# The last stage of a hybrid decoder step: accumulators, order of the second half, and how the final norm and its stores are placed

## The chip, the cores and the metric

The kernel runs on one core of one Trainium2 chip. Its engines are TensorE (PE in the profile, its weight loads PEld), VectorE (DVE), ScalarE (ACT), GpSimd (POOL) and SyncE (SP), which here only issues DMAs. The metric is the time of one execution on the device in microseconds; lower is better. Three runs of the kernel before gave 1003.35, 1006.09 and 1006.34 us, a median of 1006.09.

## The reference, cut to what matters

One step of a decoder layer over 512 prompt tokens and 8 sample tokens, 520 in all, with 1024 features: a SwiGLU feed-forward, a mixer (pooling and a state space model), a second SwiGLU feed-forward, and a last RMS norm. The change lies in the end of the second feed-forward and in the norm:

```python
h = h + 0.5 * _swiglu(_rms_norm(h, ffn2_norm), ffn2_w_gate, ffn2_w_up, ffn2_w_down)
...
return _rms_norm(h, final_norm), ...

def _rms_norm(x, g):
    y = x * rsqrt(mean(x * x, axis=-1) + EPS)
    return y * g
```

The mean runs over the 1024 features of a token, so no token of the output is known before all its features are.

## The kernel before, in words

Features lie on the 128 partitions, in 8 tiles `d` = 0 to 7 of 128 features each (`KD`); tokens lie along a row, in two halves `b` of 260 tokens (`HB`). Products are made to nearly fp32 precision by splitting both operands into a high and a low part and taking three matmuls (`mm3`, lines 116 to 119).

The feed-forward's 2816 inner features are 22 tiles, taken in chunks of 8, 8 and 6. For each chunk `rest` (lines 318 to 338) makes the gated products `g` and then multiplies them with the down-projection. For the last chunk this is `down_by_half` (lines 392 to 432): it loads and splits the weights of all eight output tiles (lines 395 to 406), and then goes through the tokens' first half and after it the second half. For each half and each output tile `part(d, b, ks)` does 6 x 3 matmuls into an accumulator `dh` in PSUM (line 417), and `done(d, b)` takes it out on DVE: line 422 scales it into `th` and line 424 adds it to `h`. Three tiles of the first half are begun without the last of the six inner tiles, while that one is still being made (lines 427 and 428).

PSUM has eight banks here: tag `ps` with two banks, tag `A` with two, and tag `BE` with two tiles of two banks. In `part` the output tiles 0 and 1, and 4 and 5, share one `BE` tile; tiles 2, 3, 6 and 7 have an `A` bank each. A buffer is given to its next user when the reads of all that was in it are done.

After each output tile `after2(d, b, hs)` (lines 526 to 538) prepares the norm. ACT squares the new `h` (`sumsq`, lines 141 to 148), DVE adds the square to `acc_last`, and ACT writes `hg`, which is `h` times the norm's gain (line 536). For the very last tile the square `sq_last` isn't added on DVE but given to TensorE, and DVE makes `hg` (lines 529 to 533). When the eighth tile of a half is through, `finish(b)` (lines 540 to 554) sums `acc_last` over the partitions with a matmul by a matrix of ones into `psl`, ACT takes the square root (line 546), and then, for each quarter of 130 tokens, DVE takes the reciprocal (line 550) and multiplies four tiles at a time (line 552), and SP stores each product (line 554): four stores of 260 KB a half, in runs of 130 floats.

The order of instructions on each engine isn't the program's. A scheduler works it out ahead of time from its own estimates of durations: what it takes to be ready first goes first, and program order decides between what is ready. `tc.keep_in_program_order(x)` sets one bound for it: `x` is issued behind the instruction that the program has just ahead of it on the same engine. On the chip each engine then works through its list in order.

Of the kernel before, what the change touches and what calls it, by code (L numbers as in the profile page):

```python
# [9 lines left out]
F32 = mybir.dt.float32  # L10
F32R = mybir.dt.float32r
AF = mybir.ActivationFunctionType
ALU = mybir.AluOpType
# [3 lines left out]
P = 128  # L17
D = 1024
# [3 lines left out]
HB = NT // 2  # L22
HALVES = (slice(0, HB), slice(HB, NT))
KD = D // P
# [38 lines left out]
def tile_trunk_step(ctx: ExitStack, tc: tile.TileContext, ins: dict, outs: dict):  # L63
    nc = tc.nc
# [7 lines left out]
    tmp = ctx.enter_context(tc.tile_pool(name="tmp", bufs=3, side="right"))  # L72
    dr = ctx.enter_context(tc.tile_pool(name="dr", bufs=1, space=DRAM))
    ps = [None]

    def bank(name):
        return ps[0].tile([P, 512], F32, tag="ps", name=name)
# [3 lines left out]
    h = vx[:, NVEC:].rearrange("p (d t) -> p d t", d=KD)  # L81

    def v(name, i, n=P):
        return vec[:n, VEC[name] + i : VEC[name] + i + 1]

    ones = cst.tile([P, P], F32, tag="ones", name="ones")
    nc.vector.memset(ones, 1.0)
    eps = cst.tile([P, 1], F32, tag="eps", name="eps")
# [7 lines left out]
    def raw_tile(name):  # L96
        if not half:
            t = raw_pair(name)
            half.extend([t[:, 1], t[:, 0]])
        return half.pop()  # L100

    def split(src, n, name, hp, nb, tags):
        hi, lo = (hp.tile([P, 1024], F32R, tag=t, bufs=nb, name=f"{t}_{name}")[:, :n] for t in tags)
        h, l = hi, lo
        if len(src.shape) == 3:
            h, l = (t.rearrange("p (j c) -> p j c", j=src.shape[1]) for t in (hi, lo))
        nc.scalar.copy(h, src)  # L107
        nc.vector.tensor_tensor(out=l, in0=src, in1=h.bitcast(F32), op=ALU.subtract)
        return hi, lo
# [3 lines left out]
        nc.sync.dma_start(out=raw, in_=src)  # L113
        return split(raw, n, name, wp, 3, ("whi", "wlo"))

    def mm3(ps, whi, wlo, xhi, xlo, start, stop, **kw):
        nc.tensor.matmul(ps, whi, xhi, start=start, stop=False, **kw)  # L117
        nc.tensor.matmul(ps, whi, xlo, start=False, stop=False, **kw)  # L118
        nc.tensor.matmul(ps, wlo, xhi, start=False, stop=stop, **kw)  # L119

    def ws(w, k, m=P):
        return w[:, k * m : (k + 1) * m]
# [18 lines left out]
    def sumsq(acc, d, hs, name):  # L141
        n = hs.stop - hs.start
        if d == 0:
            nc.scalar.activation(out=acc[:, hs], in_=h[:, d, hs], func=AF.Square)
        else:
            sq = tmp.tile([P, HB], F32, tag="ta", name=f"sq_{name}_{d}")
            nc.scalar.activation(out=sq[:, :n], in_=h[:, d, hs], func=AF.Square)
            nc.vector.tensor_tensor(out=acc[:, hs], in0=acc[:, hs], in1=sq[:, :n], op=ALU.add)
# [47 lines left out]
    class Ffn:  # L196
# [153 lines left out]
        def down(self, c, lo, hi, after):  # L350
# [3 lines left out]
            def part(d, ks):  # L354
                if d not in units:
                    units[d] = load_unit(ins[f"w{self.i}d"][d, :, lo * P : hi * P], n * P, f"{self.i}d{d}_{c}")
                    banks[d] = ps[0].tile([P, 2, 512], F32, tag="BE", bufs=2, name=f"dn{self.i}_{d}_{c}")
                wh, wl = units[d]
                for b in range(2):
                    for k in ks:  # L360
                        g = self.g[lo + k]
                        mm3(banks[d][:, b, :HB], ws(wh, k), ws(wl, k), g[:, 0, b], g[:, 1, b], k == 0, k == n - 1)
# [29 lines left out]
        def down_by_half(self, c, lo, after, wd):  # L392
            n = KF - lo
            banks, units = {}, []
            for d in range(KD):
                src, name = ins[f"w{self.i}d"][d, :, lo * P :], f"{self.i}d{d}_{c}"
                raw = raw_tile(name)[:, : n * P]
                nc.sync.dma_start(out=raw, in_=src)
                if d < 4:
                    home = (wp, 3, ("whi", "wlo")) if d < 2 else (self.wx, 2, ("shi", "slo"))  # L400
                    units.append(split(raw, n * P, name, *home))
                    continue
                hi, lw = (wd.tile([P, n * P], F32R, tag=t, bufs=KD - 4, name=f"{t}_{name}") for t in ("dhi", "dlo"))
                nc.scalar.copy(hi, raw)
                nc.vector.tensor_tensor(out=lw, in0=raw, in1=hi.bitcast(F32), op=ALU.subtract)
                units.append((hi, lw))

            def part(d, b, ks):
                if (d, b) not in banks and d % 4 < 2:
                    t = ps[0].tile([P, 2, 512], F32, tag="BE", bufs=2, name=f"dh{self.i}_{d}{b}")  # L410
                    banks[d, b], banks[d + 1, b] = t[:, 0], t[:, 1]
                elif (d, b) not in banks:
                    banks[d, b] = ps[0].tile([P, 512], F32, tag="A", bufs=2, name=f"dh{self.i}_{d}{b}")
                wh, wl = units[d]
                for k in ks:
                    g = self.g[lo + k]
                    mm3(banks[d, b][:, :HB], ws(wh, k), ws(wl, k), g[:, 0, b], g[:, 1, b], k == 0, k == n - 1)

            def done(d, b):
                hs = HALVES[b]  # L420
                t = self.wx.tile([P, 2, HB], F32, tag="tg", bufs=2, name=f"th{self.i}_{d}{b}")[:, 0]
                nc.vector.scalar_tensor_tensor(out=t, in0=banks[d, b][:, :HB], scalar=-0.5, in1=self.nx[3][:, hs],
                                               op0=ALU.mult, op1=ALU.mult)
                nc.vector.tensor_tensor(out=h[:, d, hs], in0=t, in1=h[:, d, hs], op=ALU.add)
                after(d, b, hs)

            for d in range(3):
                part(d, 0, range(n - 1))
            for b in range(2):
                for d in range(KD):  # L430
                    part(d, b, range(n - 1, n) if b == 0 and d < 3 else range(n))
                    done(d, b)
# [10 lines left out]
    for j in range(KD // 2):  # L443
        for d in (j, j + KD // 2):
            q = slice(NVEC + d * NT if d else 0, NVEC + (d + 1) * NT)
# [70 lines left out]
    last = act.tile([P, NT], F32, tag="acc", name="acc_last")  # L516
    res = []

    def before2():
# [3 lines left out]
        res.append(f2["hg"].tile([P, NT], F32, tag="rl", name="r_last"))  # L523
        return f2["hg"]

    def after2(d, b, hs):
        hg = res[0]
        if (d, b) == (KD - 1, 1):
            sq = tmp.tile([P, HB], F32, tag="ta", name="sq_last")
            nc.scalar.activation(out=sq, in_=h[:, d, hs], func=AF.Square)  # L530
            nc.vector.tensor_scalar(out=hg[:, d, hs], in0=h[:, d, hs], scalar1=v("final_norm", d), scalar2=None,
                                    op0=ALU.mult)
            finish(1, sq)
            return
        sumsq(last, d, hs, f"l{d}{b}")
        nc.scalar.activation(out=hg[:, d, hs], in_=h[:, d, hs], func=AF.Copy, scale=v("final_norm", d))
        if (d, b) == (KD - 1, 0):
            finish(0)

    def finish(b, sq=None):  # L540
        hs, hg, rl = HALVES[b], *res
        ps = bank(f"psl{b}")
        nc.tensor.matmul(ps[:, :HB], ones, last[:, hs], start=True, stop=sq is None)
        if sq is not None:
            nc.tensor.matmul(ps[:, :HB], ones, sq, start=False, stop=True)
        nc.scalar.activation(out=rl[:, hs], in_=ps[:, :HB], func=AF.Sqrt, bias=eps, scale=1.0 / D)
        cuts = (hs.start, hs.start + HB // 2, hs.stop)
        for t in (slice(cuts[0], cuts[1]), slice(cuts[1], cuts[2])):
            n = t.stop - t.start
            tc.keep_in_program_order(nc.vector.reciprocal(out=rl[:, t], in_=rl[:, t]))  # L550
            for q in (slice(0, 4), slice(4, KD)):
                nc.vector.tensor_tensor(out=hg[:, q, t], in0=hg[:, q, t],
                                        in1=rl[:, t].unsqueeze(1).to_broadcast([P, 4, n]), op=ALU.mult)
                nc.sync.dma_start(out=outs["y"][:, q, t], in_=hg[:, q, t])

    f2["ffn"].rest(before2, after2)
    for p in (ps[0], f2["st"], g2, f2["hg"], f2["wx"]):
        p.release()
# [541 lines left out]
```

## Time and profile before

| what | value |
|---|---|
| median of 3 runs | 1006.09 us |
| the profiled execution's own time | 1003.51 us |
| its span, first to last instruction | 1000.5 us |
| mean granted clock of TensorE | 0.994 |
| matmuls of the program | 7850 |
| last weights loaded for `down_by_half`, issued from | 937.11 us |
| first `dh` matmul | 943.56 us |
| stores of `y`, issued | 976.66 to 995.24 us |

Times in the profile are counted from the span's start. Rows of a timeline give start, duration, engine, line and operation, the tile written, an arrow, the tiles read, the shapes, and how many instructions are merged; in brackets how long the engine had idled just before, and whose end released it. Matmuls overlap, so their distance from start to start is their cost in a run, not their duration. A name with q behind an engine (SPq, DVEq) is that engine's sequencer. Rows of stretches give the stretch, its length, the busy time of PE, PEld, DVE, ACT and POOL, the granted clock, the busy share of the 16 DMA engines, and GB/s.

### The profile page before, as it was taken

What the parts mean: (1) busy time and instruction counts of PE and PEld (TensorE: products, weight loads), DVE (VectorE), ACT (ScalarE), POOL (GpSimd) and SP (SyncE); (2) the same over time, 40 slices, a digit from 0 to 9 for tenths busy, and PEclk for the clock granted to TensorE, in tenths of its full rate; (3) what the DMA queues carried; (4) which work ended last, traced back from release to release, by engine and by line L of the source; (5) the groups of instructions that cost most, each with busy time, mean ns of one, the idle gap of its engine ahead of it and who ended that gap; (6) DMA issues with size and microseconds to landing.
All of it is one profiled execution on the core that took longest, in us unless ns stands there. A gap on an engine that the chain in (4) does not pass through costs nothing.

```text
span 1000.5 us, 19362 instructions
## 1 busy us (share of the span) xinstructions
PE 971.7 (97%) x7850; PEld 951.4 (95%) x7850; DVE 806.9 (81%) x1408; ACT 528.7 (53%) x881; POOL 87.8 (9%) x157
## 2 busy tenths in 40 slices
PE   7999999999999999999999999999999999999994
PEld 6899999999999999999899998899999999999993
DVE  7999657996569688788979987999957999668865
ACT  7566414664145455684845235666743666436552
POOL 0000000000000000167312000100012000120000
PEclk9999999999999999999999999999999999999997
DMA  6333232323223223263334421423346333452213
GB/s 194 112 126 114 98 101 73 124 88 124 85 85 106 85 104 117 87 216 105 107 133 122 146 90 54 124 94 118 127 137 187 120 127 118 124 195 96 95 33 85
DMA packets 44072, 114.44 MB, mean 114 GB/s; under 512 B 6408, under 2 KB 15560, under 8 KB 43984
## 3 DMA queue, kind: packets, MB, share of 16 engines
q1 hardware_dynamic: 40912, 103.78, 30.7%
q0 software_dynamic: 3072, 9.44, 3.5%
q8 instruction: 61, 1.00, 0.4%
q14 instruction: 27, 0.22, 0.1%
HBM read 105.86 MB, written 7.34 MB: 113 GB/s over the span
## 4 chain that ended last, share of the span: by engine, by line
PE 88%; DVE 6%; ACT 2%; POOL 2%; issue 1%; DMA 0%; SPq 0%; DVEq 0%; ACTq 0%
PE A L119 8%; PE A L117 8%; PE A L118 8%; PE dn L117 7%; PE dn L119 7%; PE dn L118 7%; PE BE L117 6%; PE BE L119 6%; PE BE L118 6%; PE P L232 4%; PE wo L117 2%; PE wo L118 2%; PE wo L119 2%; PE inz L117 2%; PE inz L119 2%; PE inz L118 2%
## 5 line engine op out<-in xcount | busy, mean ns | idle before, releaser
L117 PE MATMUL dn<-g,whi_1d 128*128 128x260 f32 x352 | 99.3, 283 | 0.2 <-DVE td L367 0.2
L118 PE MATMUL dn<-g,whi_1d 128*128 128x260 f32 x352 | 99.5, 283 | 0.0
L119 PE MATMUL dn<-g,wlo_1d 128*128 128x260 f32 x352 | 99.4, 283 | 0.0
L367 DVE SCALAR_TENSOR_TENSOR td<-dn,r_f 128x520 f32<-128x520 f32 x40 | 27.9, 699 | 73.2 <-PE dn L119 73.2
L119 PE MATMUL dn<-g,wlo_2d 128*128 128x260 f32 x256 | 72.4, 283 | 0.0
L118 PE MATMUL dn<-g,whi_2d 128*128 128x260 f32 x256 | 72.3, 282 | 0.0
L117 PE MATMUL dn<-g,whi_2d 128*128 128x260 f32 x256 | 72.3, 282 | 0.0
L117 PEld LDWEIGHTS dn<-g,whi_1d 128*128 128x128 f32 x352 | 66.1, 188 | 0.4 <-DVE td L367 0.4
L118 PEld LDWEIGHTS dn<-g,whi_1d 128*128 128x128 f32 x352 | 66.3, 188 | 0.0
L119 PEld LDWEIGHTS dn<-g,wlo_1d 128*128 128x128 f32 x352 | 66.2, 188 | 0.0
L297 ACT COPY ac<-A 128x260 f32<-128x260 f32 x123 | 45.6, 374 | 29.3 <-PE A L119 28.0
L107 ACT CAST whi_1d<-raw_1d 128x1024 fp32r<-128x1024 f32 (+1 forms) x24 | 23.4, 980 | 67.0 <-PE dn L118 54.2
L260 DVE TENSOR_TENSOR s<-raw 128x1024 f32<-128x1024 f32 x41 | 50.0, 1220 | 3.9 <-DMA raw<-in_w2gu 3.9
L232 PE MATMUL P<-xg_f,raw 128*128 128x260 f32 x192 | 45.1, 392 | 6.2 <-DMA raw<-in_w1gu 5.4
L232 PEld LDWEIGHTS P<-xg_f,raw 128*128 128x128 f32 x192 | 36.9, 195 | 12.1 <-ACT xg_f L179 5.4
L117 PEld LDWEIGHTS dn<-g,whi_2d 128*128 128x128 f32 x256 | 48.3, 189 | 0.0
L118 PEld LDWEIGHTS dn<-g,whi_2d 128*128 128x128 f32 x256 | 48.2, 188 | 0.0
L119 PEld LDWEIGHTS dn<-g,wlo_2d 128*128 128x128 f32 x256 | 48.2, 188 | 0.0
L118 PE MATMUL wo<-catg,whi_wo 128*128 128x260 f32 x128 | 36.4, 285 | 1.3 <-DVE catg L957 1.3
L117 PE MATMUL wo<-catg,whi_wo 128*128 128x260 f32 x128 | 37.3, 292 | 0.3 <-DVE h L926 0.3
L117 PE MATMUL inz<-xh_mx,whi_inz 128*128 128x260 f32 x128 | 36.8, 287 | 0.1
L117 PE MATMUL inx<-xh_mx,whi_inx 128*128 128x260 f32 x128 | 36.4, 284 | 0.0
(1340 smaller groups left out, 3924.1 us busy)
## 6 DMA issues: line engine op xcount, KB each, us to landing
raw<-in_w2gu SPq DMA_DIRECT2D x44, 512.0 KB, 4.5
raw<-in_w1gu SPq DMA_DIRECT2D x42, 512.0 KB, 4.4
raw_1d<-in_w1d SPq DMA_DIRECT2D x16, 512.0 KB, 4.4
raw_2d<-in_w2d SPq DMA_DIRECT2D x16, 512.0 KB, 4.6
raw_wo<-in_w_out SPq DMA_DIRECT2D x12, 512.0 KB, 5.0
ab<-scr_acs SPq DMA_DIRECT2D x8, 512.0 KB, 4.8
h<-in_state_ssm SPq DMA_DIRECT2D x16, 256.0 KB, 4.2
raw_inz<-in_w_in SPq DMA_DIRECT2D x8, 512.0 KB, 3.9
```

The costliest lines, as they stand in the source:

```text
L107: nc.scalar.copy(h, src)
L117: nc.tensor.matmul(ps, whi, xhi, start=start, stop=False, **kw)
L118: nc.tensor.matmul(ps, whi, xlo, start=False, stop=False, **kw)
L119: nc.tensor.matmul(ps, wlo, xhi, start=False, stop=stop, **kw)
L232: nc.tensor.matmul(self.banks[f, u][b][:, :HB], ws(self.raw[f][:, u], j + 4 * q), xg[:, slot[q]], start=j == q == 0, stop=j == 3 and q == ...
L260: nc.vector.tensor_tensor(out=s1, in0=diag, in1=up0, op=ALU.add)
L297: nc.scalar.copy(keep, out[:, :HB])
L367: nc.vector.scalar_tensor_tensor(out=t, in0=banks[d][:, :, :HB], scalar=-0.5, in1=self.nx[3].rearrange("p (b t) -> p b t", b=2), op0=ALU.mult,
```

## The change

Four things, all in the last stage:

- In `part`, no two output tiles share a buffer any more. Odd tiles take an `A` bank, even ones a `BE` tile of which one bank is used, and tiles 2 and 3 of the first half take the two `ps` banks.
- The first matmul of each output tile of the second half, but for tile 1, is kept in program order, so these tiles follow each other.
- The norm of the first half is put in a list `todo` of six pieces (two reciprocals, four products with their stores), of which one is worked off after each of the tiles 1 to 6 of the second half. Each is kept in program order.
- In the second half the squares of tiles 6 and 7 both go to TensorE (`late`), which sums three terms for `psl`. The square root is taken in two quarters, each followed by its reciprocal, and a product covers two tiles by all 260 tokens of the half; its store has runs of 260 floats. There are four stores of 260 KB a half as before.

```diff
-    def mm3(ps, whi, wlo, xhi, xlo, start, stop, **kw):
-        nc.tensor.matmul(ps, whi, xhi, start=start, stop=False, **kw)
+    def mm3(ps, whi, wlo, xhi, xlo, start, stop, pin=False, **kw):
+        first = nc.tensor.matmul(ps, whi, xhi, start=start, stop=False, **kw)
+        if pin:
+            tc.keep_in_program_order(first)
...
             def part(d, b, ks):
-                if (d, b) not in banks and d % 4 < 2:
-                    t = ps[0].tile([P, 2, 512], F32, tag="BE", bufs=2, name=f"dh{self.i}_{d}{b}")
-                    banks[d, b], banks[d + 1, b] = t[:, 0], t[:, 1]
-                elif (d, b) not in banks:
-                    banks[d, b] = ps[0].tile([P, 512], F32, tag="A", bufs=2, name=f"dh{self.i}_{d}{b}")
+                if (d, b) not in banks:
+                    if b == 0 and d in (2, 3):
+                        banks[d, b] = bank(f"dh{self.i}_{d}{b}")
+                    elif d % 2:
+                        banks[d, b] = ps[0].tile([P, 512], F32, tag="A", bufs=2, name=f"dh{self.i}_{d}{b}")
+                    else:
+                        t = ps[0].tile([P, 2, 512], F32, tag="BE", bufs=2, name=f"dh{self.i}_{d}{b}")
+                        banks[d, b] = t[:, 0]
...
-                    mm3(banks[d, b][:, :HB], ws(wh, k), ws(wl, k), g[:, 0, b], g[:, 1, b], k == 0, k == n - 1)
+                    mm3(banks[d, b][:, :HB], ws(wh, k), ws(wl, k), g[:, 0, b], g[:, 1, b], k == 0, k == n - 1,
+                        pin=b == 1 and k == 0 and d != 1)
...
+    todo, late = [], []
+
     def after2(d, b, hs):
         hg = res[0]
+        if (d, b) == (0, 1):
+            finish(0, [last[:, HALVES[0]]])
+        elif b and todo:
+            todo.pop(0)()
+        if b and d >= KD - 2:
+            late.append(tmp.tile([P, HB], F32, tag="ta", name=f"sq_last{d}"))
+            nc.scalar.activation(out=late[-1], in_=h[:, d, hs], func=AF.Square)
+        else:
+            sumsq(last, d, hs, f"l{d}{b}")
         if (d, b) == (KD - 1, 1):
-            sq = tmp.tile([P, HB], F32, tag="ta", name="sq_last")
-            nc.scalar.activation(out=sq, in_=h[:, d, hs], func=AF.Square)
             nc.vector.tensor_scalar(out=hg[:, d, hs], in0=h[:, d, hs], scalar1=v("final_norm", d), scalar2=None,
                                     op0=ALU.mult)
-            finish(1, sq)
+            finish(1, [last[:, hs], *late])
+            while todo:
+                todo.pop(0)()
             return
-        sumsq(last, d, hs, f"l{d}{b}")
         nc.scalar.activation(out=hg[:, d, hs], in_=h[:, d, hs], func=AF.Copy, scale=v("final_norm", d))
-        if (d, b) == (KD - 1, 0):
-            finish(0)
-
-    def finish(b, sq=None):
+
+    def finish(b, sqs):
         hs, hg, rl = HALVES[b], *res
         ps = bank(f"psl{b}")
-        nc.tensor.matmul(ps[:, :HB], ones, last[:, hs], start=True, stop=sq is None)
-        if sq is not None:
-            nc.tensor.matmul(ps[:, :HB], ones, sq, start=False, stop=True)
-        nc.scalar.activation(out=rl[:, hs], in_=ps[:, :HB], func=AF.Sqrt, bias=eps, scale=1.0 / D)
-        cuts = (hs.start, hs.start + HB // 2, hs.stop)
-        for t in (slice(cuts[0], cuts[1]), slice(cuts[1], cuts[2])):
-            n = t.stop - t.start
-            tc.keep_in_program_order(nc.vector.reciprocal(out=rl[:, t], in_=rl[:, t]))
-            for q in (slice(0, 4), slice(4, KD)):
-                nc.vector.tensor_tensor(out=hg[:, q, t], in0=hg[:, q, t],
-                                        in1=rl[:, t].unsqueeze(1).to_broadcast([P, 4, n]), op=ALU.mult)
-                nc.sync.dma_start(out=outs["y"][:, q, t], in_=hg[:, q, t])
+        for k, sq in enumerate(sqs):
+            nc.tensor.matmul(ps[:, :HB], ones, sq, start=k == 0, stop=k == len(sqs) - 1)
+        cuts = (0, HB // 2, HB)
+        quarters = [slice(cuts[i], cuts[i + 1]) for i in range(2)]
+        for q in quarters:
+            nc.scalar.activation(out=rl[:, hs][:, q], in_=ps[:, q], func=AF.Sqrt, bias=eps, scale=1.0 / D)
+
+        def inverse(q):
+            tc.keep_in_program_order(nc.vector.reciprocal(out=rl[:, hs][:, q], in_=rl[:, hs][:, q]))
+
+        def out(d):
+            tc.keep_in_program_order(
+                nc.vector.tensor_tensor(out=hg[:, d : d + 2, hs], in0=hg[:, d : d + 2, hs],
+                                        in1=rl[:, hs].unsqueeze(1).to_broadcast([P, 2, HB]), op=ALU.mult))
+            nc.sync.dma_start(out=outs["y"][:, d : d + 2, hs], in_=hg[:, d : d + 2, hs])
+
+        todo.extend([lambda q=q: inverse(q) for q in quarters])
+        todo.extend([lambda d=d: out(d) for d in range(0, KD, 2)])
```

## The prediction

> **What bounds the kernel now.** I read the page first, then the chain of work that ended last over the final 16 us, then the timelines of PE, DVE and ACT from 957 us on, and last the DMA view of the two stretches in which `y` is stored.
>
> ```profile
> span 1000.5 us, 19362 instructions
> ...
> PE 971.7 (97%) x7850; PEld 951.4 (95%) x7850; DVE 806.9 (81%) x1408; ACT 528.7 (53%) x881; POOL 87.8 (9%) x157
> ```
>
> TensorE sets the pace over the whole. The change leaves its work as it is and touches only the end, so what matters is where PE waits in the last stage, and what stands behind its last weight matmul. The chain from there, in order of time (start, us, what; x2 is a pair):
>
> ```profile
> 984.76 0.13 PE dh L119
> ...
> 984.91 0.77 DVE th L422 x2
> ...
> 986.11 0.30 ACT sq_l L147
> ...
> 986.93 0.32 ACT sq_l L147
> ...
> 987.28 0.44 DVE acc_last L148
> ...
> 987.76 1.14 PE psl L543 x2
> 988.90 0.88 PE psl L545 x2
> ...
> 989.81 0.49 ACT r_last L546
> ...
> 990.32 0.98 DVE r_last L550
> ...
> 991.32 1.31 DVE hg L552 x2
> 992.63 0.89 DVE r_last L550
> ...
> 993.54 0.70 DVE hg L552
> 994.24 0.61 DVEq L1080
> ```
>
> The reader is to see a serial tail. Call T the end of the last `dh` matmul, 984.89. Then 2.87 us pass until the sums of squares reach TensorE at 987.76: two or three output tiles finish together, and their squares and adds queue one behind the other on ACT and DVE. The sum over partitions takes 2.0 us, the square root 0.5, and two rounds of reciprocal and products last until 994.85. The rest of the span, 5.65 us, is stores and the program's end. T to the last product is 9.96 us.
>
> PE also stands still twice in this stage:
>
> ```profile
> 958.67 0.28 PE L119 MATMUL dh<-g,wlo_2d 128*128 128x260 f32 x1
> 959.47 0.39 PE L117 MATMUL dh<-g,whi_2d 128*128 128x260 f32 x1 [0.52 <-DVE th L422]
> 959.70 0.28 PE L118 MATMUL dh<-g,whi_2d 128*128 128x260 f32 x1
> 959.82 0.28 PE L119 MATMUL dh<-g,wlo_2d 128*128 128x260 f32 x1
> ...
> 973.25 0.60 PE L543 MATMUL psl<-acc_last,ones 128*128 128x260 f32 x2
> ...
> 979.30 0.28 PE L119 MATMUL dh<-g,dlo_2d 128*128 128x260 f32 x1
> 980.30 0.39 PE L117 MATMUL dh<-g,dhi_2d 128*128 128x260 f32 x1 [0.73 <-DVE th L422]
> ```
>
> Starts are 0.12 apart in an unbroken run (959.70, 959.82). From 958.67 to 959.47 is 0.80, so 0.68 is lost; the next step of 0.23 loses 0.11 more. The second place loses 0.88 (979.30 to 980.30), and I add the same 0.11. Together 1.78 us. Both wait for `th`, the DVE read that gives an accumulator back. Why the second read was late is seen on DVE:
>
> ```profile
> 957.85 0.43 DVE L422 SCALAR_TENSOR_TENSOR th<-dh,r_f 128x260 f32<-128x260 f32 x1 [0.25 <-PE dh L119]
> 958.31 0.43 DVE L424 TENSOR_TENSOR h<-th,h 128x260 f32<-128x260 f32 x1
> ...
> 974.40 0.97 DVE L550 RECIPROCAL r_last<-r_last 128x130 f32<-128x130 f32 x1 [3.56 <-ACT r_last L546]
> 975.28 0.70 DVE L422 SCALAR_TENSOR_TENSOR th<-dh,r_f 128x260 f32<-128x260 f32 x2
> 975.90 1.30 DVE L552 TENSOR_TENSOR hg<-hg,r_last 128x520 f32<-128x520 f32 x2
> ...
> 979.83 0.76 DVE L422 SCALAR_TENSOR_TENSOR th<-dh,r_f 128x260 f32<-128x260 f32 x2
> ```
>
> The reciprocal of the first half held DVE's queue for 3.56 us until its square root came, and the whole norm of that half was then worked off with only two `th` let through at 975.28; the next pair came at 979.83, and PE had stopped for it.
>
> **The change, part by part.** *Accumulators and order.* Each output tile gets a bank of its own; eight tiles of a half take four or more banks in turn, and the second half starts at 0 and ends at 7. A tile is 18 matmuls of 0.12, or 2.16 us. In the second half a bank comes back three tiles (6.5 us) after it was filled, against 0.89 for its two DVE steps (957.85 to 958.74). So both stops should go: T falls by 1.78. What the pinning adds is that tile 0 of the second half may not start before tile 7 of the first, so PE can't step past a late tile. Queued behind are all remaining `dh` matmuls. What tiles 5 to 7 of the first half need is there:
>
> ```profile
> 955.69 1.90 DVE L405 TENSOR_TENSOR dlo_2d<-raw_2d,dhi_2d 128x768 fp32r<-128x768 f32 x2 [0.56 <-ACT dhi_2d L404]
> ```
>
> The last weight halves are split by 957.59, before PE would ask for any of these three tiles (958.79). Bounds for T: no gain at all if the stops only move, 1.78 as best; I take 1.78, since the two waits have one cause each and both causes are removed.
>
> *First half's norm spread.* Two reciprocals (0.97) go behind tiles 1 and 2 of the second half, four products of 520 columns (0.70) behind tiles 3 to 6, each with its store. DVE then does per tile 0.43 + 0.43 + 0.43 and one of these: 2.26 at most, 1.99 mostly, beside 2.16 of PE. It costs nothing while it stays under PE's pace with three tiles of slack; without that cover each tile would cost the excess. The last spread product stands behind tile 6, and ends about 1.24 - 0.70 = 0.5 us ahead of T, so it is not in the way of tile 7. The square root behind it can't stall DVE as it did: it has all of tile 1 to arrive, some 2 us and more.
>
> *The sum.* Only tile 7 is left behind T. Its path: hand-over 0.03, two DVE steps 0.89, then
>
> ```profile
> 958.77 0.42 ACT L144 ACTIVATE acc_last<-h 128x260 f32<-128x260 f32 x1 [2.17 <-DVE h L424]
> ...
> 973.89 0.48 ACT L546 ACTIVATE r_last<-psl,eps 128x260 f32<-128x260 f32 x1 [1.09 <-PE psl L543]
> ```
>
> a square with its hand-over, 0.45. The other two terms of the sum (the accumulator through tile 5, the square of tile 6) go through TensorE in the 1.4 us in which tile 7 is on DVE and ACT: at most 0.60 each (the pair of 973.25), hidden. If they weren't, some 0.6 would be added. Tile 7's own sum is one matmul pair, 0.64 from its start to the square root by the first half's (973.25 to 973.89), with 0.04 of hand-over. That is at full clock. In the second half of before it was not:
>
> ```profile
> 987.70:990.00 2.30, 2.00 (x4) 1.08 (x4) 0.28 (x2) 0.45 (x2) 0.00 (x0) 0.54 0.00 0
> ```
>
> Here the column behind POOL is the granted clock, 0.54, after PE had idled from 984.89 to 987.76; a pair took 0.88 and more. With a gap of half a microsecond at most the clock should hold; if not, 0.4 us come back. The square root over 130 columns is in no row: between nothing and the 0.48 of 260 columns; I take 0.37, nearer the latter, since much of a short instruction is fixed. [...] Two reciprocals in a row, 0.88 (974.40 to 975.28) + 0.97 and 0.03; the second root runs beside the first. Then four products, three times 0.61 (a pair took 1.31) and one of 0.70, 2.53, and 0.03. Sum from T: 0.03 + 0.89 + 0.45 + 0.04 + 0.64 + 0.37 + 1.88 + 2.56 = 6.86 us, against 9.96. Gain 3.10.
>
> *Stores.* The queue of SP issues all of them:
>
> ```profile
> 937.11 13.60 SPq L398 DMA_DIRECT2D raw_2d<-in_w2d  x6
> 976.66 18.58 SPq L554 DMA_DIRECT2D out_y<-hg  x8
> ```
>
> Nothing else is on it then, and the first half's four now go out one per tile, the last about 0.5 us ahead of T, done well before the second half's first. Bytes and number of the stores stay (4 of 260 KB a half); runs of 520 B become 1040 B. The DMA view of each half's stretch (9 us from 975, then 9.5 us from 991):
>
> ```profile
> q1 hardware_dynamic: 2112, 1.07, 41.9%
> ```
>
> ```profile
> q1 hardware_dynamic: 2112, 1.07, 53.9%
> ```
>
> ```profile
> 992.50:993.00 0.50, 0.00 (x0) 0.00 (x0) 0.50 (x2) 0.00 (x0) 0.00 (x0) 0.50 0.02 5
> 993.00:993.50 0.50, 0.00 (x0) 0.00 (x0) 0.50 (x1) 0.00 (x0) 0.00 (x0) 0.50 0.90 255
> ...
> 998.00:998.50 0.50, 0.00 (x0) 0.00 (x0) 0.00 (x0) 0.00 (x0) 0.00 (x0) 0.50 0.02 4
> ```
>
> Four stores keep 16 engines busy for 0.419 x 9 = 3.8 us in the first half, 0.539 x 9.5 = 5.1 in the second (last columns: share, GB/s). Data starts about 1.0 us after the first product (992.0 to 993.0), stops about 998.1, and the span ends 2.4 us later. After the change the first product is ready at T + 5.03, data runs from T + 6.0. The four come within 1.8 us, so the engines set the end: 3.7 us as in the first half, T + 9.7, and T + 12.1 is the span's end. Bounds: 1.9 us of data if a run of 1040 B cost what one of 520 B does, 5.1 if the slow rate holds; I take 3.7, the rate of the undisturbed half. Before, the span ended at T + 15.6. So behind T 3.5 us are won, 3.1 of it ahead of the stores. [...]
>
> **Sum:** 1.78 + 3.5 = 5.3 us. The profiled execution took 1003.51 us (span 1000.5, 3.0 around it), which gives 998.2. Three runs gave 1003.35, 1006.09 and 1006.34, so the profiled one stands at their low end; 5.3 off the median is 1000.8. I forecast midway, **999.5**.
>
> **The rivals.** *The order is pinned but DVE sets the pace.* If DVE waits for each square before its add (0.5 a tile, as in-order queues do), a tile costs it 2.5 to 2.8, some 0.4 more than PE, and tile 7 is read about 2.6 us late. For it: that DVE waited 3.56 us behind one reciprocal. Against: spread items fill just that wait. Gain 2.7: 1000.8 to 1003.4. *Stops move, stores stay slow.* T gains nothing, data takes 5.1 us: 5.3 - 1.8 - 1.4 = 2.1: 1001.4 to 1004.0. *It doesn't do what it says.* Only some instructions are pinned; the rest is ordered by the scheduler's own estimate, which put a reciprocal 3.56 us too early before. If squares of several tiles again bunch behind T, only the sum's 1 us and the clock's 0.9 are won: 1001.6 to 1004.2. *Slower.* The pin lets PE no longer step past a tile. If the weight halves of tiles 6 and 7 came late, PE would stand for as long as they are late; it decides from 5.3 us, and at 8.5 late (some 969 instead of 957.6) the kernel is 3.2 slower: 1006.7 to 1009.3. Against it: 3 us of reserve at tile 6 already.
>
> **How the numbers follow.** Forecast 0.68; DVE's pace 0.10; stops moved and slow stores 0.10; not done 0.08; slower 0.04. The forecast's own range is its two bases with 1 us each way, 997 to 1002; taking in the DVE and store rivals' larger part and the bounds of the stores (1.8 less, 1.4 more), 996.3 to 1003.3. About 0.3%, 3 us, is what a measurement of this kernel can tell from no change: the rivals between lie at 2 to 3 us of gain and go mostly to "same", with a little of the forecast; that gives faster 0.76, same 0.20, slower 0.04.
>
> **What would show it.** Right: no idle of PE before a `dh` row behind 958; T near 983.1; one `th` alone behind T; the last `psl` pair at clock 1.00; the span's end 12 us behind T. Wrong: a `th` that starts over 0.5 us after its tile's last matmul; a stop of PE at the first tile of the second half; stores that run for 5 us.

## The result and the profile after

The kernel after takes 997.44 us (median of 4 runs, 997.11 to 999.22), the kernel before 1004.72 (median of 4, 1002.22 to 1006.34). The ratio is 0.9937, with a 95% interval of 0.9923 to 0.9951: faster by 5 to 8 us. The forecast was 999.5.

The profiled execution of after took 999.22 us and was the slowest of its four. Its page begins:

```profile
span 997.1 us, 19372 instructions
...
PE 972.4 (98%) x7852; PEld 952.2 (96%) x7852; DVE 808.0 (81%) x1407; ACT 529.4 (53%) x883; POOL 85.5 (9%) x157
```

The span is only some 3.4 us shorter than that of before, since the last stage began 2.7 us later in it (first `dh` at 946.26, before 943.56). That is scatter from upstream, where the two kernels have the same instructions in the same order: over the fourteen profiles told of here the start lies between 943.3 and 946.5, whichever kernel ran. So I compare from the first `dh` matmul on, in two pieces: the **stage**, to the end of the last `dh` matmul, T, and the **tail**, from T to the span's end. The stage is one row of stretches of after, and one of before (columns as in the prediction: the stretch, its length, PE's busy time):

```profile
946.26:985.75 39.49, 39.49 (x329) 39.43 (x328) 29.28 (x62) 20.38 (x43) 0.00 (x0) 1.00 0.18 61
```

```profile
943.56:984.89 41.33, 40.07 (x328) 39.38 (x326) 27.08 (x57) 18.45 (x38) 0.00 (x0) 1.00 0.21 65
```

After, PE is busy in all of it; before, 1.26 us were idle, and the rest of the 1.84 between the two lies in longer busy time, the slow first matmul after a stop among it (0.23 us from its start to the next at 959.47 in before, against 0.12 in an unbroken run). Now the chain that ended last, after:

```profile
985.62 0.14 PE dh L121
...
985.77 0.44 DVE th L428
...
986.24 0.44 DVE h L430
...
986.76 0.43 ACT sq_last L542
...
987.23 0.72 PE psl L558 x2
...
987.98 0.38 ACT r_last L562
...
988.38 1.80 DVE r_last L565 x2
...
990.20 0.70 DVE hg L569
990.90 0.61 DVEq L1100
991.52 1.22 DVE hg L569 x2
```

Where before had several tiles at once (`th` x2, two squares `sq_l` with an `hg` between them), one instruction now follows the other for a single tile. The first reciprocal starts 2.63 us behind T (988.38 - 985.75; before 990.32 - 984.89 = 5.43), and the last product ends at T + 7.0 (992.74) instead of 9.96. The stores, in stretches (last three columns: granted clock, busy share of the DMA engines, GB/s):

```profile
987.20:988.00 0.80, 0.71 (x2) 0.30 (x2) 0.00 (x0) 0.02 (x1) 0.00 (x0) 1.00 0.00 0
...
991.00:992.00 1.00, 0.00 (x0) 0.00 (x0) 1.00 (x2) 0.00 (x0) 0.00 (x0) 0.50 0.11 36
992.00:992.50 0.50, 0.00 (x0) 0.00 (x0) 0.50 (x2) 0.00 (x0) 0.00 (x0) 0.50 1.02 341
...
994.50:995.00 0.50, 0.00 (x0) 0.00 (x0) 0.00 (x0) 0.00 (x0) 0.00 (x0) 0.50 0.92 316
995.00:995.50 0.50, 0.00 (x0) 0.00 (x0) 0.00 (x0) 0.00 (x0) 0.00 (x0) 0.50 0.02 4
```

And the DMA view of 987.0 to 997.1, its row of the queue:

```profile
q1 hardware_dynamic: 1088, 1.07, 31.0%
```

Half as many packets, 31% of 10.1 us: 3.1 us of all 16 engines instead of 5.1. Data runs from 991.8 to 995.0, and the span ends 11.3 us behind T, 4.3 less than before. From the last packet of `y` to the span's end it takes 1.7 to 2.0 us in the profiles with long stores, 1.9 to 2.4 in those with short ones, and 3.3 in one of these. So a difference of 0.3 us between two tails says nothing yet.

### The profile page after: what moved, and what is told of

Read it like the earlier page. It is cut to its first block, busy times and chain, and to the rows that moved or that the text cites. A ratio compares the mean times of both kernels' runs of the same rounds, so it can differ in the third digit from the quotient of the medians.

```text
span 997.1 us, 19372 instructions
## 1 busy us (share of the span) xinstructions
PE 972.4 (98%) x7852; PEld 952.2 (96%) x7852; DVE 808.0 (81%) x1407; ACT 529.4 (53%) x883; POOL 85.5 (9%) x157
## 4 chain that ended last, share of the span: by engine, by line
PE 87%; DVE 6%; POOL 2%; ACT 2%; issue 1%; DMA 1%; SPq 0%; DVEq 0%; ACTq 0%
PE A L121 8%; PE A L117 8%; PE A L120 8%; PE dn L121 7%; PE dn L117 7%; PE dn L120 7%; PE BE L117 6%; PE BE L121 6%; PE BE L120 6%; PE P L234 5%; PE wo L117 2%; PE wo L121 2%; PE wo L120 2%; PE inz L117 2%; PE inz L121 2%; PE inz L120 2%
```

## The experiments

All times below are of one execution's profile (stage, tail) or of repeated runs beside the kernel before (median, ratio with its 95% interval). Two theories stood at the start. By the prediction's each part has its own gain: the accumulators remove the first stop of PE, the spread norm the second, the pinned order and the late squares the bunch behind T. By the rival the accumulators do all of that, and spread, pins and late squares do nothing. The letters A and B of an expectation hold within it.

**The accumulators alone.** The kernel before with this part only:

```diff
-                if (d, b) not in banks and d % 4 < 2:
-                    t = ps[0].tile([P, 2, 512], F32, tag="BE", bufs=2, name=f"dh{self.i}_{d}{b}")
-                    banks[d, b], banks[d + 1, b] = t[:, 0], t[:, 1]
+                if (d, b) not in banks:
+                    if b == 0 and d in (2, 3):
+                        banks[d, b] = bank(f"dh{self.i}_{d}{b}")
...
```

> The kernel before with own accumulators alone: no pins, the first half's norm in one go, stores of 130-token runs. Measured in two stretches: first dh matmul to the last one (before 41.33 us, changed kernel 39.49) and from there to the span's end (15.66 and 11.35). Theory A, as on record: each of PE's two stops has its own cause, so only the stop at 959 goes and the one behind the norm's burst stays: 40.3 to 40.6. Theory B: the accumulators alone make the order that of the tiles and give three tiles of slack, which also covers the burst: 39.5, and one tile alone behind the last matmul. In both the first product is ready about 4.4 us behind the last matmul; with the stores as slow as before (8.5 us from there to the end) the tail is 12.9, with the first half's rate 11.6. Sum against before: A -3.6 to -5.0, B -4.6 to -5.9 us.

Measured: 997.56 us, ratio 0.9955 [0.9943, 0.9968]; stage 39.48, tail 12.52. No pin is in this kernel and the first half's norm is worked off in a burst as before, yet PE never stops. It goes through the `dh` matmuls in the same order as in after. DVE's timeline:

```profile
971.95 0.97 DVE L553 RECIPROCAL r_last<-r_last 128x130 f32<-128x130 f32 x1 [0.66 <-ACT r_last L549]
...
973.12 0.42 DVE L425 SCALAR_TENSOR_TENSOR th<-dh,r_f 128x260 f32<-128x260 f32 x1
973.45 1.30 DVE L555 TENSOR_TENSOR hg<-hg,r_last 128x520 f32<-128x520 f32 x2
974.66 0.96 DVE L553 RECIPROCAL r_last<-r_last 128x130 f32<-128x130 f32 x1
...
975.82 0.41 DVE L425 SCALAR_TENSOR_TENSOR th<-dh,r_f 128x260 f32<-128x260 f32 x1
...
978.05 0.42 DVE L425 SCALAR_TENSOR_TENSOR th<-dh,r_f 128x260 f32<-128x260 f32 x1
...
979.46 0.43 DVE L425 SCALAR_TENSOR_TENSOR th<-dh,r_f 128x260 f32<-128x260 f32 x1 [0.31 <-PE dh L119]
```

The `th` reads come singly, one a tile: they are held up between 973 and 978, by 0.8 us at most, and are back on time at 979.46, and PE, with other banks to fill, does not notice. The accumulators alone set tile order, remove both stops and the bunch, as theory B had it; the tail lies between the two named, 11.6 and 12.9.

The burst is not quite that of before: the reciprocal waits 0.66 us for its root, not 3.56, since the order on DVE changed too. How the second stop of before came about shows in the kernel's instruction lists, which give the tiles to the rows. The matmul that waited at 980.30 begins tile 7, and its `A` bank, one that no other tile shared, had been tile 3's. The row below is the last matmul of tile 3 in before:

```profile
975.84 0.28 PE L119 MATMUL dh<-g,slo_2d 128*128 128x260 f32 x1
```

It ended at 976.12, and its `th` came at 979.83, 3.7 us late. In the mixed order of before only 29 matmuls, 3.5 us, lay between tile 3 and tile 7; in tile order three whole tiles do, 6.5 us. So the norm did hold the read up, but the order decided that PE felt it. Only the first stop of before, at 959.47, was at a shared buffer: tile 0 of the second half took over that of tiles 0 and 1.

**All but the accumulators.** The kernel after with the shared banks of before (the diff above reversed); pins, spread norm, late squares and long stores stay.

> The changed kernel with the accumulators of before (two tiles share a buffer), all else kept, the pins too. Theory A: the stop of 0.8 us at the first half's end comes back, the second doesn't: 40.2 us from first to last dh matmul, tail 11.4, so 0.7 slower than the changed kernel. Rival, the order alone is what counts: pinned order takes the shared buffers late enough, 39.5 and 11.4, no difference from the changed kernel.

Measured: 1000.3 us, ratio 0.9979 [0.9970, 0.9988]; stage 42.35, tail 11.01. Both expectations of the stage were too low: it is 1.0 us longer than in before. PE's timeline, all its stops there:

```profile
961.00 0.36 PE L117 MATMUL dh<-g,dhi_2d 128*128 128x260 f32 x1 [0.95 <-DVE th L425]
...
970.40 0.39 PE L117 MATMUL dh<-g,whi_2d 128*128 128x260 f32 x1 [0.52 <-DVE th L425]
...
980.26 0.39 PE L117 MATMUL dh<-g,dhi_2d 128*128 128x260 f32 x1 [0.52 <-DVE th L425]
```

The second and the third are at a shared buffer: tile 1, and later tile 5, may not begin before the tile ahead of it in the same buffer has been read, though the bank itself is another. These reads were on time, 0.03 us or so behind the last matmul of their tile:

```profile
969.92 0.43 DVE L425 SCALAR_TENSOR_TENSOR th<-dh,r_f 128x260 f32<-128x260 f32 x1
...
979.77 0.43 DVE L425 SCALAR_TENSOR_TENSOR th<-dh,r_f 128x260 f32<-128x260 f32 x1 [0.29 <-PE dh L121]
```

The first, at 961.00, is tile 6 of the first half, which waits for the `A` bank of tile 2. So tile order and shared buffers don't go together, and no late norm is needed for that. The mixed order of before can be read as a way round these waits. Behind T this kernel ends as after does: the pins, too, put an end to the bunch, but the stops ahead of T cost 2.9 us against after.

**The spread taken back.** The kernel after, with the first half's six pieces in one go:

```diff
         if (d, b) == (0, 1):
             finish(0, [last[:, HALVES[0]]])
+            while todo:
+                todo.pop(0)()
```

> The changed kernel with the first half's two reciprocals and four products all asked for after the second half's first tile instead of one a tile. Theory A: the burst (4.5 us of DVE) makes PE wait for an accumulator again: 40.3 to 40.6 us from first to last dh matmul (changed kernel 39.49). Theory B: three tiles of slack, 6.5 us, absorb it: 39.5, and the tail stays at 11.4, as DVE has caught up by then.

Measured: 997.07 us, ratio 0.9950 [0.9938, 0.9963]; stage 39.48, tail 11.34, as in after. DVE's timeline has both reciprocals and the four products together, and a `th` between them:

```profile
970.90 1.79 DVE L567 RECIPROCAL r_last<-r_last 128x130 f32<-128x130 f32 x2 [0.55 <-ACT r_last L564]
...
972.89 0.42 DVE L428 SCALAR_TENSOR_TENSOR th<-dh,r_f 128x260 f32<-128x260 f32 x1
973.23 2.52 DVE L571 TENSOR_TENSOR hg<-hg,r_last 128x520 f32<-128x520 f32 x4
```

The spread buys nothing that shows. The reciprocal waits 0.55 us for its root, not 3.56.

**Tile 6's square back on DVE.**

```diff
-        if b and d >= KD - 2:
+        if b and d >= KD - 1:
```

> The kernel after, but tile 6's square of the second half is added on DVE as the first six, so that TensorE gets two terms for psl instead of three. Theory A: DVE has the time for one more add of 0.43 us while TensorE does tile 7, and the accumulator is done ahead of tile 7's square: tail 11.3 to 11.4 as in after, no change. Theory B (as the prediction has it, the bunch behind T was the cost): the add stands ahead of tile 7's th in DVE's queue and tile 7 comes up to 0.4 us later: tail 11.7.

Measured: 996.95 us, ratio 0.9942 [0.9922, 0.9963]; stage 39.48, tail 11.03, the first reciprocal at T + 2.64 as in after. DVE adds it ahead of time:

```profile
983.42 0.43 DVE L150 TENSOR_TENSOR acc_last<-acc_last,sq_l 128x260 f32<-128x260 f32 x1
984.13 0.43 DVE L428 SCALAR_TENSOR_TENSOR th<-dh,r_f 128x260 f32<-128x260 f32 x1 [0.28 <-PE dh L121]
```

It has 0.28 us to spare ahead of tile 7's `th`. The late square of tile 6 buys nothing that shows either.

**The second half's stores as before.** The kernel after, with runs of 130 tokens:

```diff
+        if b:
+            for q in quarters:
+                inverse(q)
+                for e in (slice(0, 4), slice(4, KD)):
+                    s = slice(hs.start + q.start, hs.start + q.stop)
+                    nc.vector.tensor_tensor(out=hg[:, e, s], in0=hg[:, e, s],
+                                            in1=rl[:, s].unsqueeze(1).to_broadcast([P, 4, HB // 2]), op=ALU.mult)
+                    nc.sync.dma_start(out=outs["y"][:, e, s], in_=hg[:, e, s])
+            return
```

> The kernel after, but the second half's final products and stores are cut as before: reciprocal, two products of 4 tiles by 130 tokens, reciprocal, two products, each with its store in runs of 520 B. The first half stays. Theory A, it is the run length that costs: the second half's four stores keep the 16 engines busy for 4.65 us, as in own_only, instead of 3.1; the first product ends at T + 4.3 instead of T + 5.17, but the end of the span comes at T + 12.4 instead of T + 11.33, 1.1 us later; median 998.5. Theory B, the stores of the kernel before were slow for something else (the idle time and the halved clock ahead of them): 3.7 us, as in the first half of before, from T + 5.2 on, and the span ends at T + 11.0 to T + 11.4: no change.

Measured: 998.72 us, ratio 0.9967 [0.9956, 0.9978]; stage 39.48, tail 12.41. The row of the queue over its last 9.4 us:

```profile
q1 hardware_dynamic: 2112, 1.07, 49.8%
```

4.7 us of data against 3.1, though it starts 0.8 us earlier: 1.1 us later at the end, as theory A had it. The runs of 260 tokens are worth 1.1 us net by the span's end, and 1.0 by the last packet (T + 9.3 instead of T + 10.3).

**The long stores alone**, in the kernel before:

```diff
-        nc.scalar.activation(out=rl[:, hs], in_=ps[:, :HB], func=AF.Sqrt, bias=eps, scale=1.0 / D)
...
+        for q in quarters:
+            nc.scalar.activation(out=rl[:, hs][:, q], in_=ps[:, q], func=AF.Sqrt, bias=eps, scale=1.0 / D)
...
+        for q in quarters:
+            inverse(q)
+        for d in range(0, KD, 2):
+            out(d)
```

> The kernel before with one part of the change alone: the square root in two quarters, both reciprocals in a row, then four products of two tiles by 260 tokens with stores in runs of 1040 B; accumulators, order and squares as before. Theory A, run length: the first product ends at T + 7.9 (T + 7.14 in before), the engines are busy for 3.1 us instead of 5.2, and the tail is 14.1 us instead of 15.67: 1.6 us less, the stage ahead of T stays at 41.3; median 1.6 us below before. Theory B: the data takes 5.2 us as in before, begins 0.8 us later, and the tail is 16.4, 0.7 us longer.

Measured: 1000.79 us, ratio 0.9986 [0.9975, 0.9996]; stage 41.25, tail 12.95. The repeated runs agree with the 1.6 us of theory A (1.8 between the medians, 0.4 to 2.5 by the interval), but this profile's tail is over 1 us shorter still. Its chain shows why:

```profile
988.49 0.70 PE psl L543 x2
989.20 0.45 PE psl L545 x2
...
989.67 0.38 ACT r_last L549
```

The two `psl` pairs take 1.15 us. In before they took 2.0 at a halved clock, after TensorE had idled just as long (2.88 against 2.87 us).

**TensorE kept busy.** So is the halved clock a property of the kernel before? First, its pause covered by 20 matmuls into a bank that the output doesn't use:

```diff
+            def fill(n):
+                t = ps[0].tile([P, 512], F32, tag="A", bufs=2, name="fill")
...
+                            nc.tensor.matmul(t[:, :HB], ws(units[7][0], 0), self.g[lo][:, 0, 1], start=k == 0, stop=k == n - 1))
...
+            f2["ffn"].fill(20)
```

> The kernel before with 20 more matmuls of 260 columns in TensorE's queue behind the last dh, into a bank that nobody reads for the output; they cover the 2.9 us in which TensorE idled ahead of psl. Theory A, the granted clock of 0.54 after this idling costs the 2.0 us of the two psl pairs: at full clock the two pairs take 0.9 to 1.2, and the tail is 14.8 to 15.0 us instead of 15.67. Theory B, the pairs wait for their operands and the clock matters little: the square root comes 0.2 us earlier at most, tail 15.5. Both: stage ahead of T 41.3.

Measured: 1002.87 us, ratio 1.0000 [0.9990, 1.0011]; stage 41.33, tail 14.58. The chain:

```profile
987.30 2.67 PE fill L424 x20
989.96 0.44 PE psl L554 x2
990.40 0.45 PE psl L556 x2
```

The pairs ran at full clock, though held up by the fillers (which started 0.86 us behind T, when a bank came free), and the profile's tail fell to a little below the 14.8 to 15.0 of theory A; the repeated runs show no gain at all. That fits if before itself has the full clock in many of its executions: there the fillers only delay `psl`. Two more profiles of before:

> The kernel before once more, unchanged, for a second profile of its end. In the first the clock was halved 3.0 us behind T, at the end of TensorE's 2.87 us of idling, and the two psl pairs took 2.0 us; in before_store260 TensorE idled 2.88 us at the same place and the pairs ran at full clock in 1.15. Theory A, the halving after such a pause is a matter of chance: this profile may show a tail of 14.6 to 14.9 us with the clock at 1.00 through psl. Theory B, it belongs to the kernel before: 15.5 to 15.8 us and 0.50 to 0.54 again. The stage ahead of T takes 41.3 us by both.

> A third profile of the unchanged kernel before. As before_again: by A either tail can come, by B 15.5 to 15.8 us.

Measured: stages 41.33 and 41.32, tails 14.57 and 14.32. The stretch of `psl` in the first of them, with 1.15 us of PE at clock 1.00:

```profile
987.90:989.20 1.30, 1.15 (x4) 0.68 (x4) 0.28 (x2) 0.31 (x2) 0.00 (x0) 1.00 0.00 0
```

The first reciprocal starts at T + 4.57 in both, where before_fill had T + 4.95 and the first profile T + 5.43. So the halving comes in some executions of one program and not in others, and the profile on which the prediction was built had caught it. How often is not measured, but the mean clocks of repeated runs give a hint: of 40 runs of before, 21 have 0.995, as these two profiles, and 15 have 0.994, as the first, and are 0.5 to 0.9 us longer. Last, 6 fillers instead of 20 (`fill(6)`):

> The kernel before with 6 filler matmuls instead of the 20 of before_fill, so that TensorE's pause is cut in two (about 0.9 and 1.2 us) and psl isn't held up by fillers. If a pause of 2.9 us is what puts the clock at risk, psl starts at T + 2.9 at clock 1.00, its two pairs take 1.15, and the first reciprocal comes at T + 4.5 (before T + 5.44, before_fill T + 4.95). If the clock has to do with something else than TensorE's own pause, the halving can still come at T + 3.0 and the reciprocal at T + 5.4.

Measured in its one profile: stage 41.31, tail 15.62, the first reciprocal at T + 5.60. In stretches:

```profile
986.30:987.40 1.10, 0.98 (x6) 0.77 (x6) 1.10 (x5) 0.64 (x2) 0.00 (x0) 1.00 0.00 0
987.40:988.40 1.00, 0.00 (x0) 0.00 (x0) 1.00 (x5) 1.00 (x4) 0.00 (x0) 1.00 0.00 0
988.48:990.60 2.12, 2.10 (x4) 1.17 (x4) 0.21 (x1) 0.12 (x1) 0.00 (x0) 0.50 0.00 0
```

The clock fell 1.1 us after the last filler, so a pause of 2.9 us in one piece is not needed for it, and six fillers are no cure. What the condition is, these runs do not show.

**A shorter chain.** The kernel after, with the last tile's `th`, `h`, square, `psl` (two banks) and root in two halves of 130 tokens:

```diff
+                if (d, b) == (KD - 1, 1):
+                    for q in (slice(0, HB // 2), slice(HB // 2, HB)):
...
+        pq = [bank(f"psl{b}{i}") for i in range(2)] if b else [bank(f"psl{b}")] * 2
...
+            for k, sq in enumerate(sqs):
+                for p, q in zip(pq, quarters):
+                    nc.tensor.matmul(p[:, q], ones, sq[:, q], start=k == 0, stop=k == len(sqs) - 1)
```

> The changed kernel with its last tile's own chain (the two DVE steps, square, sum, root) done in two column halves of 130, each sum in a bank of its own. Theory: the tail is a chain, so whatever starts the first reciprocal earlier moves all behind it: first half's steps 0.25 instead of 0.44 each, square 0.31 instead of 0.42, sum 0.2 less; first reciprocal 0.5 to 0.8 us earlier, tail 10.6 to 10.9 instead of 11.35. Rival: the four stores' 3.1 us of data or the second half's sums set the end, or more and smaller instructions eat the gain: 11.2 to 11.6.

Measured: 995.87 us, ratio 0.9940 [0.9927, 0.9952]; stage 39.48, tail 10.61. Its chain:

```profile
984.30 0.32 ACT sq_last L551
...
984.66 0.50 PE psl L573 x2
...
985.19 0.38 ACT r_last L575
...
985.59 1.80 DVE r_last L578 x2
```

The first reciprocal starts at T + 2.12, 0.5 us earlier than in after, and the tail is 0.7 shorter (0.5 by the last packet), as its theory had it. It beats before clearly and has the lowest median of all; against after, which ran beside other runs of before, the ratios can't tell it apart.

**Why the later stores of 130 tokens are slow.** stores_130, with the last 130 tokens first:

```diff
-            for q in quarters:
+            for q in quarters[::-1]:
```

> stores_130, but of the second half the last 130 tokens are made and stored first. In stores_130 the first pair of these stores moved 245 to 332 GB/s and the second 158 to 295; in the first half of before both pairs moved 243 to 330. Theory A, the place of the last 130 tokens in y is slow: now the first pair is slow (160 to 240 GB/s) and the second quick. Theory B, it is the last pair in time that is slow: the rates stand as in stores_130. Both: the four keep the 16 engines busy for 4.5 to 4.8 us; the tail is 12.2 to 12.7 us.

Measured in its one profile: tail 13.67; the queue's time is 49.2% of 8.7 us, 4.3 us. The GB/s of the last stretch, in 40 slices, in stores_130 (9.4 us) and here (8.7 us):

```profile
GB/s 0 0 0 0 0 0 0 0 0 31 292 248 314 290 294 303 285 197 9 237 252 230 166 162 186 239 243 232 175 126 20 0 0 0 0 0 0 0 0 0
```

```profile
GB/s 0 0 29 285 258 285 320 282 294 296 294 105 19 275 268 280 316 287 304 234 172 148 86 43 17 0 0 0 0 0 0 0 0 0 0 0 0 0 0 0
```

The first pair in time is quick both times, so the place in `y` is not it; but here only the end of the second pair is slow. What slows it stays open, as does the tail, which is 1.0 us longer than the most that either theory gave, though data ended hardly later behind T than in stores_130 (10.4 and 10.3 us): the program's end came 3.3 us after the last packet, in after 2.0.

## Why the prediction was right, and where not

The sum held. With the two later profiles of before as base (stage 41.33, tail 14.45), each kernel's stage and tail give a gain, and over 1002.6 us (the median of 25 runs of before) a ratio:

| kernel | stage + tail | gain | as a ratio | measured |
|---|---|---|---|---|
| after | 50.81 | 5.0 | 0.9950 | 0.9937 [0.9923, 0.9951] |
| own_only | 52.00 | 3.8 | 0.9962 | 0.9955 [0.9943, 0.9968] |
| old_banks | 53.36 | 2.4 | 0.9976 | 0.9979 [0.9970, 0.9988] |
| norm_burst | 50.82 | 5.0 | 0.9951 | 0.9950 [0.9938, 0.9963] |
| sq6_on_dve | 50.51 | 5.3 | 0.9947 | 0.9942 [0.9922, 0.9963] |
| stores_130 | 51.89 | 3.9 | 0.9961 | 0.9967 [0.9956, 0.9978] |
| before_store260 | 54.20 | 1.6 | 0.9984 | 0.9986 [0.9975, 0.9996] |
| before_fill | 55.91 | -0.1 | 1.0001 | 1.0000 [0.9990, 1.0011] |
| last_tile_split | 50.09 | 5.7 | 0.9943 | 0.9940 [0.9927, 0.9952] |

All nine lie in their intervals. With the first profile as base every ratio is 0.0012 lower, and old_banks, stores_130, before_store260 and before_fill fall outside. If the clock is halved in part of the executions, under half by the hint above, the base lies between the two, and the change is worth 5.0 to 5.6 us, of 5.3 predicted. Its parts against the later profiles: the accumulators 1.84 in the stage and 1.9 in the tail (own_only), the long stores 1.1 (stores_130) to 1.6 with the half-width roots (before_store260), the rest nothing that shows.

By the prediction's steps:

- **T falls by 1.78.** Measured 1.84. The size was right, and so were both waits as read: a shared buffer for the first, a `th` held up by the norm for the second. The step "the two waits have one cause each and both causes are removed" failed, since the parts of the change are not one for each wait. The accumulators alone give tile order, and with it 6.5 us between tile 3 and tile 7, more than the 3.7 by which the read was late in before (in own_only it is 0.8 at most). own_only has the burst and no stop; old_banks spreads the norm and has three.
- **The pin and the spread cost nothing.** They cost nothing, as said, and they bring nothing; own_only has neither and the same stage. The slower rival found no late weights, and DVE's pace set nothing: the last `th` starts 0.02 us behind T.
- **T to the last product, 6.86.** Measured 6.99. Up to the first reciprocal 2.63 instead of 2.45, of which 0.11 is the `psl` pair (0.75 from its start to the root, not 0.64); the reciprocals and products came 0.05 shorter. The root over 130 columns took 0.38, where 0.37 was taken. Half the columns thus saved 0.10 of the 0.48; ACT's copies in before took 0.37 us over 260 columns and 0.62 over 512.
- **A gain of 3.10 on this chain.** Of the 9.96 it was taken from, 0.87 is the halved clock, which two further profiles of before don't have (first reciprocal at T + 4.57 instead of 5.43). The row with 0.54 was read as a trait of the kernel; it was a trait of that execution, and of some others. Against the two later profiles the chain gains 2.1 (9.11 - 6.99).
- **Stores' data 3.7 us.** The mis-sized term: it took 3.1, since runs of 1040 B move at 341 to 352 GB/s where those of 520 B had some 290. The rate was carried over from the short runs, and so the longer run was given no price of its own. The quickest slice of these stores moved 379 GB/s.
- The last two errors have opposite signs. The tail of before was taken 1.2 us longer than in the later profiles (15.67 and 14.45), 0.9 of it for the clock; that of after was put 0.8 too long (12.1 and 11.33), 0.6 of it for the data. That they nearly cancel, so that 5.3 came out near 5.0, is luck. The rest of the way from 999.5 to 997.44 is the base: with more runs the median of before fell from 1006.09 to 1004.72, and to 1002.56 in the longest series.

## What to carry to other kernels

When PE stops for a read, find out which tile's buffer the waiting matmul takes over, and how many matmuls lie between the two. Two tiles in one buffer make PE wait even for a read that is on time (0.52 us idle at each such place in old_banks), and here they went with an order that put only 3.5 us between two tiles where tile order puts 6.5, and that bunched at the end. With a buffer each, stops and bunch both went; pinning tile order around the old buffers ended the bunch, but made the stage 1.0 us longer than before. Count the last stores by their run length, not by their bytes alone (260 KB four times took 3.1 us in runs of 1040 B and 3.8 to 5.1 in runs of 520 B). And before a term of a sum is taken from a single execution, look whether it hangs on the granted clock: a second profile costs little and moved this sum by 0.9 us here.

## What the runs showed of the hardware

- Stores of 260 KB from 128 partitions: in runs of 520 B, 2112 packets took 3.8 us (first half of before) to 5.1 us of all 16 engines, in runs of 1040 B 1088 packets took 3.1 us (after, and 36.5% of 8.6 us in before_store260). Fewer, longer packets take longer each (0.046 against 0.029 us and more) and win.
- The granted clock fell to 0.50 at T + 3.0, + 4.9 and + 4.2 us in three profiles of one program (before, before_again, before_again2), and in before_fill6 1.1 us after the last of six fillers; in before_fill it was 1.00 in every slice up to 992.94, 2.1 us after the last `psl` matmul. TensorE's pause ahead of `psl` was 2.87 us in before and 2.88 in before_again2 and before_store260, and of these three only in before did `psl` run at the halved clock, so the length of the pause alone doesn't tell them apart. What sets the time of the fall was not shown.
- The kernel after is done with TensorE by T + 2.2, ahead of the earliest of these falls; its own clock fell at T + 5.1.
